# Swapping the quadrants of an 8192 x 8192 matrix by DMA: many small DMAs of 8 KB packets in the place of few large ones of 16 KB packets

## The chip, the cores and the metric

The kernel runs on one core of one Trainium2 chip. The metric is the device time of one execution in microseconds (us). Nothing is computed: the kernel is a copy from HBM to HBM, carried by the 16 DMA engines of the core.

## The reference

```python
def setup_inputs():
    return {"x": np.random.randn(8192, 8192).astype(np.float32)}

def reference(x):
    return np.fft.ifftshift(x)
```

With even sizes, `ifftshift` moves each row by 4096 rows and each column by 4096 columns, both modulo 8192. So row `r` of the output is row `(r + 4096) % 8192` of the input with its two halves exchanged. One half row is 4096 float32, 16,384 bytes, and contiguous in both tensors. There are 16,384 half rows, 268.4 MB; each is read once and written once.

## The kernel before

The kernel has a single loop over `row`, 16 steps of 512 rows (`ENGINES * per`, that is 16 x 32). A step issues two DMAs straight from the input tensor to the output tensor: one on SyncE's queue (SP) for the left halves of the output rows, one on ScalarE's queue (ACT) for the right halves. Each DMA moves 512 half rows, 8 MB. In all there are 32 DMAs, 16 on each queue.

The list `dims` sets the order of the half rows in a DMA. Its outermost dimension counts 16 neighbouring rows, the middle one counts 32 steps of 16 rows, the innermost is the half row. The outermost dimension is the one that is dealt out to the 16 DMA engines, so engine `e` moves rows `e`, `e + 16`, `e + 32` and so on of the step, one 16 KB packet for each half row, and at the end of its share a 4 byte packet that adds to the DMA's semaphore.

No semaphore is written in the source. The Tile framework adds them: it hands out eight semaphores in turn (four to each queue), and from the fifth DMA of a queue on, each DMA waits for the one that used its semaphore before. In the profile the two DMAs have line L30 (the call `queue.dma_start`); the framework's waits and barriers at the end have L59 (the end of the `with` block around the kernel's call), and the constants and barriers at the start have L48.

Of the kernel before, what the change touches and what calls it, by code (L numbers as in the profile page):

```python
# [1 line left out]

# [4 lines left out]


ENGINES = 16


@with_exitstack
def kernel(
    ctx: ExitStack,
    tc: tile.TileContext,
    x: bass.AP,
    out: bass.AP,
):
    nc = tc.nc
    R, C = x.shape  # L20
    hr = R // 2
    hc = C // 2


    per = 32
    dims = [[C, ENGINES], [ENGINES * C, per], [1, hc]]
    for row in range(0, R, ENGINES * per):
        src_row = (row + hr) % R
        for queue, h in ((nc.sync, 0), (nc.scalar, hc)):
            queue.dma_start(  # L30
                out=bass.AP(out.tensor, out.offset + row * C + h, dims),
                in_=bass.AP(x.tensor, x.offset + src_row * C + hc - h, dims),
            )


# [1 line left out]
_INS = ['x']  # L37
_OUTS = [((8192, 8192), 'float32')]


def kernel(**inputs):
    import numpy as _np
    import concourse.bacc as _bacc
    import concourse.tile as _tile
    from concourse import mybir as _mybir
    from concourse.bass_utils import run_bass_kernel_spmd as _run

    nc = _bacc.Bacc("TRN2", target_bir_lowering=False, num_devices=1)  # L48
    arrays, args = {}, []
    for name in _INS:  # L50
        a = _np.ascontiguousarray(inputs[name])
        if a.dtype.kind in "iu":
            a = a.astype(_np.int64)
        arrays[f"in_{name}_dram"] = a
        args.append(nc.dram_tensor(f"in_{name}_dram", a.shape, _mybir.dt.from_np(a.dtype), kind="ExternalInput").ap())
    for i, (shape, dtype) in enumerate(_OUTS):
        dt = _mybir.dt.from_np(_np.dtype(dtype))
        args.append(nc.dram_tensor(f"out_{i}_dram", shape, dt, kind="ExternalOutput").ap())
    with _tile.TileContext(nc) as tc:  # L59
        kernel(tc, *args)  # L60
    r = _run(nc, [arrays], core_ids=[0])
    got = tuple(r.results[0][f"out_{i}_dram"] for i in range(len(_OUTS)))
    return got[0]
```

## Time and profile before

| | |
|---|---|
| three executions | 821.38, 823.50 and 823.81 us, median 823.5 us |
| profiled execution: span from first to last instruction | 821.2 us |
| data moved | 268.44 MB read, 268.44 MB written |
| mean rate over the span | 327 GB/s (read and write together 654 GB/s) |
| DMA packets | 16,896, of them 512 of 4 bytes |
| DMA issues | 16 on SP, 16 on ACT, 8192 KB each |
| issue to landing | median 204.0 us on SP, 204.1 us on ACT |

The profiled execution has no time of its own beside its span: the times of the three executions stand without a mark for the profile. The span lies 0.2 us under the lowest of them and 2.3 us under the median.

No compute engine has work here. The rows that matter are the DMA engines' busy share and GB/s in 40 slices, the DMA queues, and the issues. "SPq" and "ACTq" are the sequencers that issue the DMAs. The trace also holds one record for each DMA packet (queue, start, duration, size), which the page only sums up. Packets that follow each other on one engine can be chained by their times, since each starts 3 to 4 ns before the one ahead of it ends.

### The profile page before, as it was taken

How to read it: one execution, taken by the hardware profiler on the slowest of the kernel's cores; microseconds unless marked ns; L12 is line 12 of the kernel's file. 1: busy time of each engine (PE TensorE's matmuls, PEld its weight loads, DVE VectorE, ACT ScalarE, POOL GpSimd, SP SyncE). 2: the span in 40 equal slices, each digit the busy share in tenths (PEclk: the TensorE clock that was granted, in tenths of full speed). 3: DMA queues.
4: the chain of work that ended last, by engine and by line, in shares of the span. 5: the costliest groups of instructions: out<-in, count | busy, mean ns of one | idle time of the engine just before them, and what ended most of it. 6: DMA issues, size and time to landing. Idle time of an engine off the chain costs nothing. (4 is left out here: it accounts for less than half of the span.)

```text
span 821.2 us, 77 instructions
## 1 busy us (share of the span) xinstructions
POOL 0.2 (0%) x4
## 2 busy tenths in 40 slices
POOL 0000000000000000000000000000000000000000
DMA  8999999999999999999999999999999999999998
GB/s 296 333 324 329 331 328 334 330 330 329 327 330 329 331 326 332 332 327 328 330 330 330 330 323 330 324 330 330 332 326 329 330 322 333 329 329 327 330 329 276
DMA packets 16896, 268.44 MB, mean 327 GB/s; under 512 B 512, under 2 KB 512, under 8 KB 512
## 3 DMA queue, kind: packets, MB, share of 16 engines
q1 hardware_dynamic: 8448, 134.22, 50.2%
q10 hardware_dynamic: 8448, 134.22, 49.0%
HBM read 268.44 MB, written 268.44 MB: 654 GB/s over the span
## 5 line engine op out<-in xcount | busy, mean ns | idle before, releaser
L48 POOL MEMSET const-bfloat16-1.0<- 128x1 bf16 x1 | 0.1, 102 | 0.0
L48 POOL MEMSET const-uint8-127<- 128x1 uint8 x1 | 0.1, 102 | 0.0
L48 POOL MEMSET const-float32-0.0<- 128x1 f32 x1 | 0.1, 99 | 0.2 <-issue 0.2
L48 POOL MEMSET const-float32-1.0<- 128x1 f32 x1 | 0.1, 99 | 0.0
## 6 DMA issues: line engine op xcount, KB each, us to landing
out_dram<-in_x_dram ACTq DMA_DIRECT2D x16, 8192.0 KB, 204.1
out_dram<-in_x_dram SPq DMA_DIRECT2D x16, 8192.0 KB, 204.0
```

What stands on the lines that cost most here:

```text
L48: nc = _bacc.Bacc("TRN2", target_bir_lowering=False, num_devices=1)
```

## The change

A DMA now covers one step of 16 half rows, 256 KB, in the place of 512 half rows. The loop has 512 steps and issues 1024 DMAs, 512 on each queue. The option `max_dma_last_dim=PACKET` cuts each half row into two packets of 8192 bytes. The loop stands in a critical section of the Tile framework, in which the framework adds no semaphores: all DMAs add 16 to one semaphore, `copied`, and SyncE waits once, after its last issue, until it has reached 16 x 1024. Which engine moves which half row stays as it was, and so do the order of the rows and the share of the two queues.

```diff
 ENGINES = 16
+PACKET = 8192
...
+    dims = [[C, ENGINES], [1, hc]]
-    per = 32
-    dims = [[C, ENGINES], [ENGINES * C, per], [1, hc]]
-    for row in range(0, R, ENGINES * per):
-        src_row = (row + hr) % R
-        for queue, h in ((nc.sync, 0), (nc.scalar, hc)):
-            queue.dma_start(
-                out=bass.AP(out.tensor, out.offset + row * C + h, dims),
-                in_=bass.AP(x.tensor, x.offset + src_row * C + hc - h, dims),
-            )
+    with tc.tile_critical():
+        copied = nc.alloc_semaphore("copied")
+        n = 0
+        for row in range(0, R, ENGINES):
+            src_row = (row + hr) % R
+            for queue, h in ((nc.sync, 0), (nc.scalar, hc)):
+                queue.dma_start(
+                    out=bass.AP(out.tensor, out.offset + row * C + h, dims),
+                    in_=bass.AP(x.tensor, x.offset + src_row * C + hc - h, dims),
+                    max_dma_last_dim=PACKET,
+                ).then_inc(copied, 16)
+                n += 1
+        nc.sync.wait_ge(copied, 16 * n)
```

## The prediction

> **What bounds the kernel now.** I read the page first: the slices, then the queues.
>
> ```profile
> DMA  8999999999999999999999999999999999999998
> GB/s 296 333 324 329 331 328 334 330 330 329 327 330 329 331 326 332 332 327 328 330 330 330 330 323 330 324 330 330 332 326 329 330 322 333 329 329 327 330 329 276
> DMA packets 16896, 268.44 MB, mean 327 GB/s; under 512 B 512, under 2 KB 512, under 8 KB 512
> q1 hardware_dynamic: 8448, 134.22, 50.2%
> q10 hardware_dynamic: 8448, 134.22, 49.0%
> HBM read 268.44 MB, written 268.44 MB: 654 GB/s over the span
> ```
>
> The 16 DMA engines are busy in every slice; the two queues add up to 99.2% of the 16 engines' span. So no issue, wait or semaphore starves them: the time is the sum of what the packets take. Next I read the packet records. The 16,384 packets of 16 KB take 13,027 us in all, 795 ns each, 1024 x 795 = 814 us per engine. They are not alike. The shortest take 608 to 611 ns, and 32% lie there; the others reach from 613 to 1889 ns. The floor is what an engine can do (1024 x 611 = 626 us); the 184 ns above it are waiting for memory. Both bounds are in the kernel at once: about a third of the packets run at the engine's pace, the rest at the memory's.
>
> Then the waits of SP's queue, and the issues of the first 3 us:
>
> ```profile
> SPq L59 <- DMA out_dram<-in_x_dram: 166.8, 2, 119.1
> SPq L30 <- DMA out_dram<-in_x_dram: 134.4, 12, 51.3
> ...
> L30 SPq DMA_DIRECT2D out_dram<-in_x_dram x4: 617/638/44336, 0.7 to 2.8; - x4
> L30 ACTq DMA_DIRECT2D out_dram<-in_x_dram x3: 660/877/900, 0.7 to 2.3; - x3
> ```
>
> Three issues pass at once, with 33 packets per engine each; SP's fourth is held for 44.3 us, until the ring is drained far enough. So about 99 packets per engine and queue fit ahead. The 12 waits at L30 are the framework's, four DMAs back: while they last, three others are queued. They cost nothing now.
>
> Last, the windows in which the 4 byte semaphore packets go out, against the stretches between them. Their place is from the packet records: 32 of them, two per engine, within 6 to 8 us, about every 51 us. Columns: stretch, length, POOL busy, clock, DMA share, GB/s. First five and one late window with them, then five stretches without.
>
> ```profile
> 50.00:57.00 7.00, 0.00 (x0) 1.00 0.99 321
> 101.00:108.00 7.00, 0.00 (x0) 1.00 0.96 316
> 152.00:159.00 7.00, 0.00 (x0) 1.00 1.00 330
> 203.00:210.00 7.00, 0.00 (x0) 1.00 1.02 332
> 254.00:261.00 7.00, 0.00 (x0) 1.00 1.01 330
> ...
> 661.00:670.00 9.00, 0.00 (x0) 1.00 0.99 319
> ```
>
> ```profile
> 57.00:101.00 44.00, 0.00 (x0) 1.00 1.00 331
> 108.00:152.00 44.00, 0.00 (x0) 1.00 1.00 331
> 159.00:203.00 44.00, 0.00 (x0) 1.00 1.00 330
> 210.00:254.00 44.00, 0.00 (x0) 1.00 1.00 330
> 261.00:305.00 44.00, 0.00 (x0) 1.00 1.00 327
> ```
>
> All 15 windows with semaphore packets (114 us together, 315 to 339 GB/s) have a mean of 325.9 GB/s, the 14 stretches between them 329.7. I come back to this difference: it is the only place where the trace shows what a semaphore packet does to its neighbours.
>
> **The change part by part.** *More semaphore packets.* Before there are 32 DMAs on 16 engines, 32 such packets per engine; after, 1024 per engine, 992 more. One has a record of 9 ns, and its successor starts 3.5 ns before it ends: 5.5 ns of engine time, 992 x 5.5 = 5.5 us. From below: if memory sets the pace in that moment, nothing. From above: the windows lose (329.7 - 325.9) / 329.7 = 1.15% of 114 us, 1.3 us for 30 packets per engine, 44 ns each, and 992 x 44 = 43 us. That end is uncertain, since windows of this length differ by up to 24 GB/s among themselves; the packet that follows a semaphore packet takes 806 ns, 11 ns over the mean, where 16 KB packets scatter by some 200 ns. I take the packet record, 5.5 us, and keep 0 and 43.
>
> *Halves cut in two.* 1024 more packets per engine. The trace has seven packets of 8 KB (instruction fetch, before the copy starts), at 307 ns; two of them are 614 ns, against 611 for one of 16 KB. That is 3 ns per half row, 3.1 us, where the engine sets the pace; in the memory's share nothing. With the 32% of packets at the floor: 1.0 us, ends 0 and 3.1. What halving does to the memory's 184 ns no row shows; it is a rival below, on both sides.
>
> *More issues.* 512 per queue in the place of 16. The unheld issues took 0.62 to 0.90 us with 33 packets per engine; the new ones have three. Taken whole, 512 x 0.90 = 461 us on ACT and 512 x 0.64 = 328 us on SP, on sequencers that have 814 us for it. Cost nothing; the cover is the ring's 99 packets, about 33 of the new DMAs ahead. It would show only from 814 / 512 = 1.59 us per issue. The new instructions are themselves fetched by DMA: seven 8 KB packets for the 77 instructions now would make 90 for 992 more, at 307 to 493 ns on 16 engines 1.7 to 2.8 us. Those seven mostly belong to the start, so I take 0 and keep 2.8.
>
> Here a rule speaks against the change. The Trainium skill, "DMA: Bandwidth & Descriptors", section "Measured", says to batch DMAs to 1 MiB and more, from a fit (for DMAs issued by GpSimd) of some 2.0 us fixed per DMA; the new ones have 256 KB. Paid one after the other, by that estimate, 1024 x 2.0 us would be 2048 us; hidden behind queued packets it would be nothing.
>
> The rows decide for hidden: DMAs overlap by the ring's depth, as now, where one takes 204 us to land and the engines still stay busy.
>
> *The framework's waits go.* 134.4 us on SP, hidden as said: gain 0. Next after them comes the ring's own limit, which holds the issues as it does now. *The one wait at the end* is last on SP, nothing but the closing barrier is behind it, and ACT doesn't wait. It takes the place of the waits at L59 for the same last packets. The section's entry and exit: the barriers at start and end fit in 0.7 us each, so 0 to 1.4 us more, taken as 0.5.
>
> *Edges.* The span less 268.44 MB at 329.7 GB/s (814.2 us) is 7.0 us. The engines' shares don't change, so neither does the uneven end; 0.
>
> Sum: 5.5 + 1.0 + 0 + 0.5 = +7.0 us on the span of 821.2; the median is 2.3 us above that span, so I add to the median: 823.5 + 7.0 = 830.5 us. With all low ends 823.5; with 43, 3.1, 2.8 and 1.4 together 874.
>
> **The rivals.** *All hidden (same).* Two thirds of the packets wait for memory, so 7 us of engine time could go into the 184 ns: 823 to 825. For it: the engines' floor of 626 us leaves room. Against: after each short delay an engine has only the same memory to catch up with, and the windows tend to the loss.
>
> *Memory is better used (faster).* The two queues take turns on each engine packet by packet, so turns become 8 KB long, and requests to the same part of memory may block each other for a shorter time. Place: every packet above the floor. It decides if the mean 8 KB packet falls under 395 ns, (795 - 5.5) / 2, the semaphore's share taken off. Price: the rate in slices reaches 334 GB/s: 268.44 / 0.334 + 7.0 = 811 span, 813; the best semaphore window has 339: 801. For it: the first microseconds, 4 to 6, run at 410 GB/s, so 330 is no hard limit. Against: that is when one queue alone supplies the engines; mixing the queues in any grain ends it, and the addresses per engine stay the same.
>
> *Each semaphore packet holds the engine (slower than forecast).* It now follows every two packets of a queue instead of 32. At 44 ns it gives 823.5 + 43 = 866; it decides once the hold is above about 10 ns, where the loss passes 10 us. For it: 325.9 against 329.7. Against: 806 ns after it is hardly above 795, and 773 before it is below.
>
> The Trainium skill, "DMA: Bandwidth & Descriptors", section "Queues, rings and completion order", says that the increment lands only after every earlier write of that engine, over all its queues; were the engine to stand still for that, this rival would be right, and no row shows it standing still.
>
> *The option does not cut, or the sequencers become the bound:* the first would leave 16,384 data packets and only the semaphores' 5.5 us; the second needs issues over 1.59 us.
>
> **How the numbers follow.** A measurement of this kernel can tell about 0.3%, 2.5 us, from no change. Forecast, small cost of 2.5 to 15 us (826 to 839): 0.36. Hidden, 821 to 826: 0.18. Memory better used, under 821: 0.29, with 0.05 of it under 801. Semaphores hold, or issues bind, over 839: 0.17, with 0.07 of it over 866. So the range is 801 to 866, the likeliest case's own 826 to 839; faster 0.29, same 0.18, slower 0.53.
>
> **What would show it.** Right: 49,152 packets, 16,384 of them under 512 B; both queues again at 99% together; 8 KB packets with a mean of 395 to 405 ns; 512 issues per queue of 256 KB, landing about 33 x 1.6 = 53 us after issue, with issues held near 1.6 us by the ring. Wrong: a DMA share below 9 in slices (issues bind), records of semaphore packets or gaps of tens of ns (they hold), or a mean under 395 ns with GB/s above 334 (memory better used). A landing time of some 6 us would mean that the limit counts DMAs, three or four per queue, not packets.

## The result and the profile after

The changed kernel takes 830.94 us (median, 829.27 to 834.0), the kernel before beside it 822.94 us. The ratio is 1.0108, 95% interval 1.0078 to 1.0137: slower by 1.1%, clear of the 0.3%. The profiled execution took 831.17 us with a span of 829.4, against 821.2 before: +8.2 us where the sum said +7.0.

The page of the changed kernel, the lines that answer to those of before (slices, packets, queues, memory, issues with size and median landing time):

```profile
GB/s 281 313 321 324 322 318 321 328 328 323 326 326 319 333 325 329 326 331 328 324 325 329 322 333 328 332 332 322 326 329 333 328 324 331 327 325 332 328 333 266
DMA packets 49160, 268.57 MB, mean 324 GB/s; under 512 B 16384, under 2 KB 16384, under 8 KB 16384
q1 hardware_dynamic: 24576, 134.25, 49.7%
q10 hardware_dynamic: 24576, 134.25, 49.5%
HBM read 268.44 MB, written 268.44 MB: 647 GB/s over the span
out_dram<-in_x_dram ACTq DMA_DIRECT2D x512, 256.0 KB, 41.4
out_dram<-in_x_dram SPq DMA_DIRECT2D x512, 256.0 KB, 41.9
```

49,152 packets on the two queues, both together at 99.2% as before, 512 issues per queue: the change does what it says, and neither an issue nor a wait binds. The packet records seem to confirm that the semaphore packets are the cost. They are 9 ns each and take 9.2 us per engine in place of 0.3, 8.9 us more where the span grew by 8.2, and the data packets take 813.3 in place of 814.2 us.

But the slices contradict it. A cost per packet would lower all of them alike. Here the first ones run at 313 to 324 GB/s, and from the middle on they look like those of before. The windows say it in numbers (stretch, length, POOL, clock, DMA share, GB/s); first before, then after:

```profile
0.00:10.00 10.00, 0.20 (x4) 1.00 0.81 275
10.00:50.00 40.00, 0.00 (x0) 1.00 1.00 326
50.00:100.00 50.00, 0.00 (x0) 1.00 0.99 329
100.00:200.00 100.00, 0.00 (x0) 1.00 1.00 330
200.00:300.00 100.00, 0.00 (x0) 1.00 1.00 329
```

```profile
0.00:10.00 10.00, 0.20 (x4) 1.00 0.77 256
10.00:50.00 40.00, 0.00 (x0) 1.00 0.99 312
50.00:100.00 50.00, 0.00 (x0) 1.00 1.00 323
100.00:200.00 100.00, 0.00 (x0) 1.00 1.00 322
200.00:300.00 100.00, 0.00 (x0) 1.00 1.00 326
...
700.00:800.00 100.00, 0.00 (x0) 1.00 1.00 330
```

Each window's loss is the difference in rate times its length over 329 GB/s: 0.6 us in the first 10, then 1.7, 0.9, 2.4 and 0.9, together 5.9 us from 10 to 300 us. All of 300 to 800 us gives 0.6. (These windows explain 7.1 of the 8.2 us; rates are whole GB/s, and one of them over 100 us is 0.3 us. The first window is the least sure, since a packet is counted whole where it starts. Counted by the ends of the packet records, the changed kernel is 0.2 us behind the one before at 10 us, 5.8 at 300 and 7.2 at 818.) So the loss is a slow start of some 300 us, in which the engines are as busy as ever.

### The profile page after: what moved, and what is told of

It reads as the page before. It is cut to its first block, busy times and chain, and to the rows that moved or that the text cites. A ratio compares the mean times of both kernels' runs of the same rounds, so it can differ in the third digit from the quotient of the medians.

```text
span 829.4 us, 1074 instructions
## 1 busy us (share of the span) xinstructions
POOL 0.2 (0%) x4
```

## Experiments

All ratios are to the kernel before, measured on the same chip, with 95% intervals. The sets of runs were taken on different chips, so ratios are compared, not times. The windows come from one profiled execution of each kernel, the ratios from all its executions.

Theory A in the expectations prices a semaphore packet at its whole record, 9 ns; the prediction had taken 5.5 ns.

### What the parts do

**Small DMAs with 16 KB packets** (edits are against the changed kernel unless something else is said; `...` stands for lines left out).

```diff
-PACKET = 8192
+PACKET = 16384
```

> The changed kernel with packets of 16 KB again: 1024 DMAs of 16 half rows, 1024 semaphore packets per engine, half rows not cut. Theory A (each of the 992 added semaphore packets takes its 9 ns of engine time, about 8.9 us, and cutting the half rows is free): ratio to the kernel before 1.010, like the changed kernel, with the loss spread evenly over the span. Theory B (cutting the half rows costs, the semaphore packets hide in the wait for memory): ratio 1.000 to 1.002. Theory C (the loss is a slow start, since in the changed kernel the stretch up to 200 us runs at 323 GB/s and later ones at 327 to 331): a start at 312 to 323 GB/s here too if small DMAs make it, at 329 if the cut makes it.

Ratio 1.0094 (1.0062 to 1.0126). Nearly all of the loss is there without the cut, which contradicts theory B; and in the profiled execution it is not even, which contradicts theory A. The windows of this kernel:

```profile
10.00:50.00 40.00, 0.00 (x0) 1.00 1.00 310
50.00:100.00 50.00, 0.00 (x0) 1.00 1.01 319
100.00:200.00 100.00, 0.00 (x0) 1.00 1.00 326
200.00:300.00 100.00, 0.00 (x0) 1.00 1.00 328
300.00:400.00 100.00, 0.00 (x0) 1.00 1.00 329
400.00:500.00 100.00, 0.00 (x0) 1.00 1.00 331
```

From 300 us on it runs as fast as the kernel before, although half of all its packets are semaphore packets. This execution took 827.15 us, the least of nine with a median of 831.29, so its windows show only about half of the loss; where the other half lies was not profiled.

**The section alone** (from the changed kernel, with the DMAs of before).

```diff
-PACKET = 8192
+PACKET = 16384
+PER = 32
...
-    dims = [[C, ENGINES], [1, hc]]
+    dims = [[C, ENGINES], [ENGINES * C, PER], [1, hc]]
...
-        for row in range(0, R, ENGINES):
+        for row in range(0, R, ENGINES * PER):
```

> The kernel before, its 32 DMAs of 8 MB and 16 KB packets, issued from the critical section with one semaphore and one wait at the end. All theories: ratio 1.000, within 0.002; the framework's waits at four DMAs back were hidden, and the section's entry and exit are under 1 us. A time above by 2 us or more would mean that the section or the single semaphore carries a part of the loss.

Ratio 0.9985 (0.9964 to 1.0006). Section, single semaphore and single wait cost nothing that can be measured.

**Four steps in a DMA**, the same with 4 in the place of 32.

> As the section-only kernel, but 256 DMAs of 64 half rows (4 per engine and DMA), 16 KB packets, 256 semaphore packets per engine, 224 more than before. Theory A: 224 x 9 ns = 2.0 us, ratio 1.0025. Theory B: 1.000. Theory C: a quarter to none of the slow start, 0 to 2 us.

Ratio 1.0003 (0.9983 to 1.0024). This alone doesn't part the theories, since the 1.0025 of theory A lies just outside the interval; its windows from 10 to 200 us are at 322 to 328 GB/s, most of the way back from the slow start. By the packet records ACT's queue is 2.3 half rows per engine ahead of SP's at 20 us here; the next part says why that matters.

**Twice the semaphore packets** (from the kernel before; the source offsets move by `part` too, and each queue has its own semaphore).

```diff
+    half = hc // 2
+    dims = [[C, ENGINES], [1, half]]
...
+            for part in (0, half):
...
+                    out=bass.AP(out.tensor, out.offset + row * C + h + part, dims),
...
```

> The changed kernel with each DMA cut in two, 2048 DMAs of 16 packets of 8 KB, so 2048 semaphore packets per engine, one behind every data packet; two semaphores, one per queue, so that neither passes 16384. Theory A: 2016 x 9 ns = 18.1 us over before, ratio 1.022. Theory B: as the changed kernel, 1.010. Theory C: as the changed kernel, 1.010, the loss in the first 200 us again. If the sequencers bind (1024 issues per queue at 0.65 us are 666 us, held under 814), DMA share falls below 9 in slices and the ratio goes beyond 1.03.

Ratio 1.0071 (1.0047 to 1.0095), not 1.022. The records show another 9.2 us of semaphore packets per engine, and the data packets give it back: their mean is 392.6 ns, against 397.1 in the changed kernel. This is what ends theory A. At the 5.5 ns of the prediction it would be 2016 x 5.5 = 11.1 us, 1.013, outside the interval too. A packet record's time does not add to the span here: the packets beside it, which take 795 ns on average where the shortest 16 KB packet takes 608, get shorter by as much.

### Where the slow start comes from

In the kernel before, one queue is ahead of the other. The view of the first issues shows it: microseconds from issue to landing (minimum, median, maximum) of the one DMA that each queue issues first. Before, SP and then ACT; then the changed kernel, ACT and then SP:

```profile
DMA to landing us min/median/max: 51.6/51.6/51.6
DMA to landing us min/median/max: 56.5/56.5/56.5
```

```profile
DMA to landing us min/median/max: 3.1/3.1/3.1
DMA to landing us min/median/max: 3.7/3.7/3.7
```

The leader is 4.9 us ahead before, 0.6 us after. Counted in packet records, the leading queue is 3.6 half rows per engine ahead at 20 us and 3.3 at 800 us in the kernel before; in the changed one 0.3 to 0.5 throughout. An engine's half rows are 16 rows apart, so before the two queues were some 58 rows apart, and now both halves of the same rows are under way together.

**ACT 64 rows behind SP**, all else as in the changed kernel.

```diff
+    behind = 64
...
-        for row in range(0, R, ENGINES):
-            src_row = (row + hr) % R
-            for queue, h in ((nc.sync, 0), (nc.scalar, hc)):
+        for step in range(0, R, ENGINES):
+            for queue, h, back in ((nc.sync, 0, 0), (nc.scalar, hc, behind)):
+                row = (step - back) % R
+                src_row = (row + hr) % R
```

> The changed kernel, but ACT's queue goes through the rows 64 rows (4 half rows per engine) behind SP's, and ends with the rows it left out. Number and size of DMAs and packets as in the changed kernel. Theory D (the lead of one queue over the other: in the kernel before the queue that starts first is 3.6 half rows per engine ahead through the whole run, in the changed one 0.4, so that both halves of one row are under way together): the lead in rows is back, the slow start goes, ratio 1.000 to 1.003. Theory E (small DMAs start the engines in a worse order, whatever the rows): as the changed kernel, 1.009 to 1.011, 312 to 323 GB/s up to 200 us. Theory A (9 ns for each semaphore packet): 1.010, evenly spread.

Ratio 1.0059 (1.0032 to 1.0085). In the profiled execution the slow start is gone:

```profile
10.00:50.00 40.00, 0.00 (x0) 1.00 0.99 330
50.00:100.00 50.00, 0.00 (x0) 1.00 1.00 329
100.00:200.00 100.00, 0.00 (x0) 1.00 0.99 330
```

The slow start isn't the size of the DMAs, then, nor the order they give to the engines, but which rows the two queues are on. Theory D said 1.003 at most, though; something of 0.3% to 0.8% is left. In the profiled execution, 2.2 us over the span of before, most of it lies between 300 and 800 us.

**First step large, the rest small** (16 KB packets, 960 small DMAs, not the 992 of the expectation; the reverse has `row >= 512`).

```diff
+    small = [[C, ENGINES], [1, hc]]
+    large = [[C, ENGINES], [ENGINES * C, 32], [1, hc]]
+    is_large = lambda row: row < 512
...
+            dims = large if is_large(row) else small
...
-                    max_dma_last_dim=PACKET,
...
+            row += ENGINES * 32 if is_large(row) else ENGINES
```

> The first step is one DMA of 8 MB on each queue as in the kernel before, all the rest are DMAs of 16 half rows (992, 16 KB packets), in the section with one semaphore. 961 semaphore packets per engine, 994 with the one of each large DMA. Theory D: the large DMAs set a lead of some 3.6 half rows that stays, ratio 1.000 to 1.003, rate 326 to 330 GB/s from 10 us on. Theory E: the same, since the start is the large DMA's. A third one, F (small DMAs slow the engines while they are young in the run for a reason of issue or ring, not of the start): slow up to 200 us once the large DMAs have ended at about 50 us, ratio 1.006. Theory A: 1.010.

Ratio 0.9982 (0.9964 to 1.0000): 960 DMAs of 256 KB and 15,392 semaphore packets, and nothing lost.

```profile
10.00:50.00 40.00, 0.00 (x0) 1.00 1.00 330
50.00:100.00 50.00, 0.00 (x0) 1.00 1.00 326
100.00:200.00 100.00, 0.00 (x0) 1.00 1.00 330
```

The lead falls from 3.6 to some 1.5 half rows after the large DMAs have ended at about 50 us and stays there, and the rate holds.

> The reverse: the first 512 rows in 64 DMAs of 16 half rows, the other 15 steps in DMAs of 8 MB, 16 KB packets, section with one semaphore. 62 semaphore packets per engine. Theories D and E: the lead of 0.4 half rows, or the bad order, is set by the start and outlives it, so the slow start up to 200 us is there although most of it runs in large DMAs, ratio 1.006 to 1.010. Theory F: slow only up to 50 us, ratio 1.003. Theory A: 1.0005.

Ratio 1.0088 (1.0058 to 1.0119): the whole loss, from 32 small DMAs on each queue. They are done by about 53 us (16.8 MB at 315 GB/s); the slow start lasts on under large ones, with a lead of 0.5 to 0.9 half rows by the packet records, and is over by 300 us. (The 62 semaphore packets of the expectation are those added; 94 per engine are in the kernel.)

```profile
10.00:50.00 40.00, 0.00 (x0) 1.00 0.99 315
50.00:100.00 50.00, 0.00 (x0) 1.00 1.00 319
100.00:200.00 100.00, 0.00 (x0) 1.00 1.00 323
200.00:300.00 100.00, 0.00 (x0) 1.00 1.00 327
300.00:400.00 100.00, 0.00 (x0) 1.00 1.00 329
```

**ACT 2048 rows behind SP**, as with 64.

> As the kernel with 64 rows between the queues, but with 2048. Theory D: the two halves of a row are far apart in time, no slow start, ratio 1.000 or below. Theory E: as the changed kernel, 1.009 to 1.011. If the distance in address between the queues matters in another way, it may differ from the one with 64 rows to either side.

Ratio 1.0082 (1.0051 to 1.0113), a miss for theory D. Its start is better than the changed kernel's (326, 325 and 327 GB/s up to 200 us), but its later windows stay at 327 to 329. So the distance matters in more ways than zero or not.

**Large DMAs without the lead.** The section-only kernel, SP beginning 64 rows further on (the blocks also split where source or output wraps round).

```diff
+    for queue, first in (("sp", 64), ("act", 0)):
+        at, end, parts[queue] = first, first + R, []
+        while at < end:
+            stop = min(at + 512, end, (at // hr + 1) * hr)
+            parts[queue].append((at % R, (stop - at) // ENGINES))
+            at = stop
...
```

> Large DMAs and 16 KB packets (the section-only kernel, ratio 0.9985), but SP begins 64 rows further on and ends with the first 64 rows; 17 or 18 DMAs per queue. In that kernel ACT's first DMA lands 5 us before SP's, a lead of some 3.6 half rows per engine, 58 rows; now the two queues are on nearly the same rows. Theory D (slow while both halves of the same rows are under way in the young run): the slow start is there with large DMAs, 310 to 323 GB/s up to 200 us, ratio 1.005 to 1.010. Theory E (the order that small DMAs give to the engines at the start): 329 GB/s from 50 us on, ratio 0.998 to 1.001. A reader should note that if SP leads in this run instead, the distance is 8 half rows and nothing is slow.

Ratio 1.0080 (1.0046 to 1.0114). ACT's first DMA lands at 53.1 us, SP's at 57.8 us, so ACT leads in time, by 3.4 to 3.8 half rows per engine in the packet records, and its rows are now within ten of SP's.

```profile
10.00:50.00 40.00, 0.00 (x0) 1.00 1.00 315
50.00:100.00 50.00, 0.00 (x0) 1.00 0.99 320
100.00:200.00 100.00, 0.00 (x0) 1.00 1.00 319
200.00:300.00 100.00, 0.00 (x0) 1.00 1.00 325
...
500.00:600.00 100.00, 0.00 (x0) 1.00 1.00 330
```

This is the strongest of the runs. No packet is cut, no small DMA is there (33 in all), and the changed kernel's slow start and its loss appear, by a shift of rows and the one more DMA that it makes.

**All on one queue**, the section-only kernel with `nc.sync` for both halves.

> The section-only kernel with all 32 DMAs on SP's queue, left and right halves in turn, so each engine works off one stream and the two halves of a row are 32 half rows of an engine apart. Theory D: no slow start. If the 410 GB/s of the first microseconds were what a single queue gives, the time would be near 268.44 / 0.41 + 7 = 662 us; if it is only the filling of buffers at the start, 1.00.

Ratio 1.0053 (1.0027 to 1.0079).

```profile
4.00:6.00 2.00, 0.00 (x0) 1.00 1.18 442
6.00:8.00 2.00, 0.00 (x0) 1.00 0.90 295
```

The high rate in the first microseconds is no rate that one queue can hold. (A DMA share of 1.18 shows that such a short window counts packets that end after it.) And the start is slow here (319, 320 and 322 GB/s up to 200 us), where theory D as it was written expected none. What this kernel has in common with the slow ones is that the 16 engines work on one group of neighbouring rows at a time, not on two. "Not both halves of a row" doesn't fit this run. "Two places apart" fits it, and the starts of most others; the kernel with four steps in a DMA (322 GB/s from 10 to 50 us at a distance of 2.3 half rows) lies between. This wider form was made after the fact and has no run of its own, and that one queue starts slowly for a reason of its own is not ruled out.

### The cut

> The kernel with ACT 64 rows behind SP and DMAs of 16 half rows, but with packets of 16 KB in the place of 8 KB. The rows between the queues took the slow start away (330 GB/s from 10 to 200 us) and left a ratio of 1.006. Theory G (what is left there is the cut into 8 KB packets, in the steady part): here 1.000, within 0.002. Theory H (what is left comes with small DMAs, semaphore packets or the first 10 us): 1.005 to 1.007 here too.

```diff
 (ACT 64 rows behind SP)
-PACKET = 8192
+PACKET = 16384
```

Ratio 1.0032 (1.0011 to 1.0053), between the two theories; its windows are even, 327 to 328 GB/s from 10 us on.

> The kernel whose first step is one DMA of 8 MB per queue (ratio 0.998 with 16 KB packets in the small DMAs), with packets of 8 KB in the small ones. Theory G: 1.004 to 1.006. Theory H: 0.998 to 1.000, as with 16 KB.

```diff
 (first step large, the rest small)
+                    max_dma_last_dim=2 * PACKET if is_large(row) else PACKET,
```

Ratio 1.0021 (1.0000 to 1.0043), between them again, and inconclusive alone. There are three pairs that differ only in the cut: 1.0108 against 1.0094, 1.0059 against 1.0032, 1.0021 against 0.9982. No pair was measured side by side, each kernel only beside the one before. The differences are 0.0014, 0.0027 and 0.0039, all to the same side, with a mean of 0.0027, about 2 us. Each pair's intervals overlap or touch, so this is an estimate, not a shown cost.

No kernel is shown to beat the one before: the two fastest, at 0.9982 and 0.9985, have intervals that reach 1.

## Why the prediction was right, and where it was not

The time was right (830.5 forecast, 830.94 measured), and so was the direction. That the number fits so well is luck: the main term of the sum was wrong, and a missing one made up for it.

*Semaphore packets, +5.5 us, with 43 as the upper end.* Wrong. The record of 9 ns is right, and the records grew by 8.9 us. But doubling them added nothing, and 930 more of them per engine behind a large first step gave 0.9982, where 5.5 ns each would have been 5.1 us, 1.006. The step that failed is the choice of the record over the lower end of 0. A half row takes 184 ns more than the shortest ones do, and time taken by semaphore packets comes off that; that it is waiting for memory is the prediction's reading, and no run shows where it is spent. The windows that hinted at 44 ns don't bear it out: 930 packets at 44 ns would be 41 us, and the same windows of the section-only kernel, with the same number of semaphore packets, have 327.3 GB/s against 328.7 between them, about a third of the difference. In the changed kernel, data packets after a semaphore packet take some 383 ns, those after a data packet some 405. The Trainium skill says in "DMA: Bandwidth & Descriptors", section "Queues, rings and completion order", that the increment lands only behind all earlier writes of its engine. No run here shows when it lands; by the packets that follow, the engine doesn't stand still for it.

*The cut, +1.0 us, ends 0 and 3.1.* The three pairs give about 2 us, inside the ends, but that is an estimate, and the working behind the 1.0 isn't confirmed. Its 307 ns is the time of four of the seven 8 KB packets; the others took 451 to 493. And in the changed kernel about 65% of the 8 KB packets lie within 2% of the shortest, where 34% of the 16 KB packets did, while two halves together take 794 ns against 795. So the share of packets at the floor was no fixed share of the time.

*Issues, 0.* Right. The added instructions brought 8 fetches during the copy, where the upper end of 2.8 us had counted 90. The issues are held by the ring, at a median of 1.48 us on SP and 1.49 on ACT. The landing time was 42 us, not 53: at 1.6 us per DMA some 26 DMAs of three packets are ahead, 78 packets, where I had read 99 from the issues that passed at once. The rule to batch DMAs to 1 MiB, which spoke against the change in the Trainium skill, "DMA: Bandwidth & Descriptors", section "Measured", would have been the wrong reason to expect a loss: 256 KB DMAs behind a large first step cost nothing (0.9982). The rule stands there over a table for copies from HBM to SBUF issued by GpSimd; the fit of 2.0 us is in the same page's section "Anatomy of one DMA — SWDGE (gpsimd) path".

*Waits, section, +0.5 us.* Not contradicted: the section alone is 0.9985 (0.9964 to 1.0006), and 0.5 us is too little to be measured.

*Edges, 0, and "the addresses per engine stay the same".* Here is the missing term. The addresses per engine stay, but not which of them are under way together on the two queues. An 8 MB DMA gives the queue that starts first 3.6 half rows before the other comes in (first packets at 2.2 and 5.1 us); a small one gives it a fraction of one (2.4 and 3.4 us). I had seen the sign of it in the first microseconds, where one queue alone supplied the engines, and read it only as a rate. The lead was an effect of the DMA size that nothing in the source says. The slow start that follows costs 5.9 of the 8.2 us between 10 and 300 us. The ratios agree only in part. With a large first step the changed kernel goes from 1.0108 to 1.0021, which takes most of the loss away; with 64 rows between the queues it goes to 1.0059, which takes away about half.

*The rival "memory is better used"* had the right place, the sharing of memory by the two queues, and the wrong sign. One argument for it, the 410 GB/s of the first microseconds, is no rate that lasts: the one-queue kernel starts at 442 and still ends at a ratio of 1.0053.

*Open.* Why the slow start heals within 300 us although the lead doesn't change was not tried. The records show one thing that does change: the 16 engines drift apart. In the kernel with SP 64 rows further on, the 16 semaphore packets of one of ACT's DMAs start within 1.2 us of each other at 53 us, 2.5 at 313 and 4.2 at 619, where an engine takes 1.6 us for a half row of each queue. So they leave their one group of 16 rows. This can't be the whole of it, since in the kernel with small DMAs first they are 3 to 4 us apart at 108 us and the rate is still 323 GB/s. What rows that lie together share in the memory was not tried either; no run here looks behind the rates. And the 64 and 2048 row distances leave 0.3 to 0.8% that the lead of the large DMAs doesn't.

## What to carry to other kernels

Look at the slices in time before believing a cost per packet: a cost that the records confirm to the microsecond was not the cause, since a cost per packet is even and the loss was not. Here packets took longer than their shortest time anyway, and small overheads went into that; what counted was which addresses were under way together. So when DMAs are made smaller, check what order and lead the large ones had given to the queues. A total that comes out right says little of its terms: take each away by itself.

## What was not expected of the hardware

The first few DMAs decide for 300 us: 32 small DMAs per queue at the start cost as much (1.0088) as all of them small (1.0094), and one large one per queue at the start saves it (0.9982). And the engines work through a semaphore packet behind every 8 KB packet, 32,768 in all, at no more cost than with half as many (1.0071 against 1.0108).
